# Layer 1's last output share cut at 256 tokens instead of 384

## The chip, the core and the metric

The kernel runs on one core of a Trainium2 chip. The metric is device time in microseconds for one execution. The core has a matrix engine (PE, with its weight loads shown as PEld), a vector engine (DVE), a scalar engine (ACT), GpSimd (POOL), and SyncE (SP), which here issues every DMA. Each engine works through its own instructions in order and waits on semaphores for the others.

## The reference

Two layers act on 512 latent tokens (a grid of 8 rows by 64 columns) and 256 context tokens, of width 1024. A layer normalises and modulates its input, projects it once, and splits the columns among three groups of heads. A is differential attention, B is grouped-query attention, and C is attention to a neighbourhood in the grid plus all context tokens. Each group's result is multiplied by a gate; the results are joined, projected by `w_out`, scaled by `gt` and added to the residual:

```python
yn = neighbourhood_attend(qn, kn, vn.reshape(b, s, C_HEADS, HEAD_DIM), kn_c, vn_c, nat_rpb[l], rows)
yn = yn * jax.nn.silu(gn)
y = jnp.concatenate([ya, yb, yn], axis=-1) @ w_out[l]
...
x = x + gt[:, None] * y
```

After layer 1 only the latent tokens are returned, all of them in float32.

## The kernel before

**Layout.** Activations lie with features on the 128 partitions and tokens along the free axis. Tokens are numbered so that 8 neighbours in a grid column stand together. A float32 product is made of three matmuls: every operand is split into a high and a low part (`yT["h"]`, `yT["l"]` for the joined results, `whi`, `wlo` for the weights), and high x high, high x low and low x high are summed in one PSUM tile. Of the 1024 rows of the joined result, row tiles 0 to 4 belong to groups A and B and tiles 5 to 7 to group C.

**Group C.** `attn(l, "C")` takes the 512 queries in four batches of 128, `j` = 0 to 3, six heads each. To keep a batch's window of keys within 256 tokens, batch `j` < 3 holds tokens 128j + 64 to 128j + 191, and batch 3 holds tokens 448 to 511 and then 0 to 63. This order of queries, 64 to 511 and then 0 to 63, is called the query order here. For each head: scores (L775), bias and maximum on DVE (L824), exponential on ACT (L841), the split into two float16 halves on ACT and POOL (L861, L862), a transpose by DMA from SP into one of four `pt` buffers (L864), and the product with the values on PE (`stage_PV`, L897 and L898, called PV). After three heads DVE divides and joins (L936 to L940), and after six it multiplies by the gate (L942). Then `y_turn` transposes the batch on PE into a PSUM tile `yt` (L618), ACT copies the high part into `yT` (L622) and DVE makes the low part (L623). Batch 3, whose tokens lie at both ends, does this in two pieces of 64 tokens.

**The output of layer 1.** It is made in three steps, all with the residual in `st["part"]`, two tiles (stB, bigC) of four blocks of 128 features. `out_parts` (L1097 to L1099, evacuated at L1127) adds the share of groups A and B for all 512 tokens while group C runs. `out_head` then adds group C's share for tokens 64 to 447, which are the batches 0 to 2: for each of eight feature blocks nine matmuls of 384 tokens into a tile `oh` (`out_n`, L1152 to L1154), an evacuation on DVE (L1163) and a store (L1164). `out_tail` does the same for the first and last 64 tokens after batch 3: four blocks share one PSUM tile `ot`, 36 matmuls of 128 tokens, four evacuations into a tile of their own (L1176), and one store (L1178), twice. `op`, `oh`, `ot` and the projections all draw on one PSUM pool, `psP`, of two buffers; `yt` of group C and the PV tiles draw on another.

**Order.** The Python code issues the program in an order of its own, and a planner then fixes each engine's order: it plays the program through with modelled durations and, whenever an engine is free, takes the instruction that is ready and most urgent. Urgency is the place in the program, less an offset that a few functions are given (stage_S 400). `fill` deals `out_parts` and `out_head` out between the steps of `attn`. By the pace that `both` computes (32 steps of fill, 7 of them kept for the end, over 28 steps of attention), `out_parts` ends with the last but one step, and the first `out_head` is issued in the last one, after the last batch's `y_turn`. So the heads stand behind all of group C in the program, and run earlier only where the planner finds PE free and their inputs there. The order on each engine, SP's included, is then fixed: on the chip an instruction whose input is late holds up what stands behind it.

## Time and profile before

| what | us |
|---|---|
| median of 3 runs | 922.99 (919.12 to 923.62) |
| profiled execution | 921.41 |
| its span, first to last instruction | 919.6 |
| PE busy in the span | 824.1 (90%) |
| DVE busy | 681.9 (74%) |
| ACT busy | 593.1 (64%) |
| POOL busy | 544.1 (59%) |

The profile is of one execution. Times in it count from the start of the span. A line of the timeline gives the start, the duration, the engine and the source line, the operation with output and inputs by the program's names, the shape, how many instructions were merged, and in brackets the idle time of the engine ahead of it with what ended that. "L864" is line 864 of the kernel. A PE row with `128*128 128x384` is a matmul of a full weight tile with 384 tokens. SPq rows are the issue of DMAs by SP.

### The profile page before, as it was taken

The page shows a single profiled execution, that of the slowest core. Times are in us where ns is not written, and L with a number is a line of the kernel's source. Part 1 is how long each engine was busy: PE and PEld are TensorE (multiplying, and loading weights), DVE is VectorE, ACT ScalarE, POOL GpSimd, SP SyncE. Part 2 cuts the span into 40 slices and gives each one's busy share as a digit, 9 for nine tenths or more (in the row PEclk, how much of TensorE's full clock was granted, in tenths as well). Part 3 has the DMA queues.
Part 4 walks back from the last instruction along what each step waited for, and adds up shares of the span by engine and source line. Part 5 has one row for each costly group of instructions (what it writes and reads, how often), then busy time and mean ns, then how long its engine had stood idle before and what let it go on. Part 6 is the DMA issues. An engine that isn't in the chain of part 4 may idle for free. (4 is left out here: it accounts for less than half of the span.)

```text
span 919.6 us, 17947 instructions
## 1 busy us (share of the span) xinstructions
PE 824.1 (90%) x6386; PEld 705.7 (77%) x6386; DVE 681.9 (74%) x1306; ACT 593.1 (64%) x1269; POOL 544.1 (59%) x503
## 2 busy tenths in 40 slices
PE   6898988896998899896999989989959999987988
PEld 3687877795987688784778879978848878875667
DVE  4985787988778866557755798789977976876743
ACT  5334577785887687577663445478758888878630
POOL 1638855899698565434421036939988886654310
PEclk9999998998999999998999989999979999998999
DMA  9924895645879997998798723784547789999642
GB/s 325 320 88 127 202 198 151 139 102 136 190 156 212 223 213 178 223 262 217 145 232 245 246 76 92 173 206 98 123 131 188 133 199 255 205 233 250 129 87 88
DMA packets 307193, 165.46 MB, mean 180 GB/s; under 512 B 256544, under 2 KB 275232, under 8 KB 306976
## 3 DMA queue, kind: packets, MB, share of 16 engines
q1 hardware_dynamic: 307104, 164.33, 74.5%
q8 instruction: 50, 0.82, 0.4%
q14 instruction: 39, 0.32, 0.1%
HBM read 86.55 MB, written 15.47 MB: 111 GB/s over the span
## 5 line engine op out<-in xcount | busy, mean ns | idle before, releaser
L862 POOL TENSOR_TENSOR hl<-p,hl 128x768 f16<-128x768 f32 (+3 forms) x138 | 205.4, 1492 | 170.7 <-ACT hl L861 159.0
L679 PE MATMUL proj<-whi,bigL 128*128 128x384 f32 (+1 forms) x592 | 203.0, 344 | 8.5 <-DVE tb L602 5.1
L680 PE MATMUL proj<-wlo,bigL 128*128 128x384 f32 (+1 forms) x592 | 199.6, 337 | 0.8 <-POOL wlo L92 0.7
L681 PE MATMUL proj<-whi,bigL 128*128 128x384 f32 (+1 forms) x592 | 196.7, 334 | 0.0
L841 ACT ACTIVATE p<-sc,nb,gsc 128x768 f32<-128x768 f32 (+3 forms) x200 | 166.3, 845 | 10.9 <-DVE p L857 4.6
L827 DVE TENSOR_REDUCE mx<-sc 128x1 f32<-128x768 f32 (+2 forms) x128 | 118.6, 931 | 30.3 <-PE sc L775 30.3
L861 ACT CAST hl<-p 128x768 f16<-128x768 f32 (+3 forms) x144 | 104.4, 725 | 46.4 <-DMA pt<-hl 29.9
L679 PEld LDWEIGHTS proj<-whi,bigL 128*128 128x128 f32 x592 | 115.0, 194 | 18.9 <-DVE tb L602 7.2
L680 PEld LDWEIGHTS proj<-wlo,bigL 128*128 128x128 f32 x592 | 115.6, 195 | 3.9 <-POOL wlo L92 1.5
L681 PEld LDWEIGHTS proj<-whi,bigL 128*128 128x128 f32 x592 | 114.5, 194 | 2.7 <-issue 1.6
L92 POOL TENSOR_TENSOR wlo<-raw,whi 128x768 fp32r<-128x768 f32 (+1 forms) x44 | 82.8, 1889 | 31.7 <-ACT whi L89 28.1
L89 ACT CAST whi<-raw 128x768 fp32r<-128x768 f32 (+1 forms) x104 | 80.1, 779 | 25.3 <-DMA raw<-in_w_in_dram 11.1
L897 PEld LDWEIGHTS <-pt 128*128 128x128 f16 x736 | 66.4, 100 | 36.8 <-DMA pt<-hl 23.2
L679 PE MATMUL proj<-whi,bigC 128*128 128x384 f32 (+2 forms) x224 | 75.6, 337 | 1.0 <-ACT xn L462 1.0
L92 DVE TENSOR_TENSOR wlo<-raw,whi 128x768 fp32r<-128x768 f32 (+1 forms) x60 | 61.5, 1028 | 19.4 <-ACT whi L89 18.1
L680 PE MATMUL proj<-wlo,bigC 128*128 128x384 f32 (+2 forms) x224 | 74.3, 332 | 0.0
L163 POOL TENSOR_TENSOR rsqb<-rsqb,half 128x12 f32<-128x12 f32 (+2 forms) x25 | 68.5, 2739 | 9.7 <-DVE rsqb L162 8.8
L681 PE MATMUL proj<-whi,bigC 128*128 128x384 f32 (+2 forms) x224 | 73.6, 331 | 0.0
L898 PEld LDWEIGHTS <-pt 128*128 128x128 f16 x736 | 66.8, 100 | 4.6 <-issue 2.4
L775 PE MATMUL sc<-bigL 128*128 128x512 f16 (+4 forms) x184 | 46.5, 314 | 18.5 <-ACT p L841 18.1
L897 PE MATMUL pv<-vA,pt 128*128 128x128 f16 (+2 forms) x424 | 52.1, 230 | 12.1 <-DMA pt<-hl 12.1
L829 ACT ACTIVATE nb<-mx,lnp,gsc 128x1 f32<-128x1 f32 (+1 forms) x104 | 39.9, 385 | 33.3 <-DVE mx L827 22.5
(327 smaller groups left out, 2038.6 us busy)
## 6 DMA issues: line engine op xcount, KB each, us to landing
raw<-in_w_in_dram SPq DMA_DIRECT2D x64, 384.0 KB, 3.9
adw<-in_w_ada_dram SPq DMA_DIRECT2D x68, 256.0 KB, 3.5
raw<-in_w_out_dram SPq DMA_DIRECT2D x16, 384.0 KB, 4.5
raw<-in_w_in_dram SPq DMA_DIRECT2D x16, 256.0 KB, 3.0
g_d<-tb SPq DMA_DIRECT2D x20, 192.0 KB, 2.8
gt<-g_d SPq DMA_DIRECT2D x18, 192.0 KB, 3.6
hl<-in_w_ada_dram SPq DMA_DIRECT2D x12, 256.0 KB, 4.8
pt<-in_w_ada_dram SPq DMA_DIRECT2D x12, 256.0 KB, 4.9
```

Source lines behind the costliest of these rows:

```text
L89: self.nc.scalar.copy(out=hi, in_=raw2)
L92: self.share("W").tensor_tensor(out=lo, in0=raw2, in1=hi.bitcast(F32), op=ALU.subtract)
L163: G.tensor_tensor(out=y, in0=x, in1=half[:, 0:n], op=ALU.pow)
L679: PE.matmul(ps, lhsT=xh, rhs=hi, start=(kt == 0), stop=False)
L680: PE.matmul(ps, lhsT=xh, rhs=lo, start=False, stop=False)
L681: PE.matmul(ps, lhsT=xl, rhs=hi, start=False, stop=(kt == KT - 1))
L827: V.tensor_reduce(out=mx[:, 0:ns], in_=ps[:, 0:w * ns].rearrange("p (a b) -> p a b", b=w), axis=AX.X, op=ALU.max)
L841: A.activation(out=p[:, w * x:w * x + w], in_=u["ps", i][:, w * x:w * x + w], func=AF.Exp, bias=u["nb", i][:, x:x + 1], scale=lc[l]["sc"][ ...
L861: A.copy(out=hl[:, 0:n], in_=p)
L862: lo_eng.tensor_tensor(out=hl[:, n:2 * n], in0=p, in1=hl[:, 0:n], op=ALU.subtract)
L897: PE.matmul(po[r, :], lhsT=pt[:, b, r], rhs=V_[:, vt, c0:129], start=first, stop=False)
L898: PE.matmul(po[r, 0:65 - c0], lhsT=pt[:, nb + b, r], rhs=V_[:, vt, c0:65], start=False, stop=stop)
```

## The change

In layer 1 group C's result is kept in query order: batch `j` goes to columns 128j of `yT`, batch 3 in one piece. `out_head` takes columns 0 to 255 (batches 0 and 1, tokens 64 to 319) and waits for these two in the program; `out_tail` takes columns 256 to 511 (tokens 320 to 511 and 0 to 63). In the tail two feature blocks share one PSUM tile, each evacuated in two pieces (192 and 64 tokens) into the residual itself, right after its matmuls, and each pair of blocks is stored by two DMAs. The output tensor is in query order, and the host turns it back.

```diff
             if j > 3:
                 spans = [(0, 128, 128 * (j - 4))]
+            elif l + 1 == DEPTH:
+
+                spans = [(0, 128, 128 * j)]
             elif j < 3:
                 spans = [(0, 128, 128 * j + 64)]
...
-                    while any((l, "C", j) not in turned for j in range(3)):
+                    while any((l, "C", j) not in turned for j in range(2)):
...
-        ps = psP.tile([128, 512], F32, tag="p", name="oh")[:, 0:384]
-        out_n(ps, l, db, lambda t: t[:, 64:448], False)
-        dst = st["part", db // 4][:, db % 4, 64:448]
+        ps = psP.tile([128, 512], F32, tag="p", name="oh")[:, 0:256]
+        out_n(ps, l, db, lambda t: t[:, 0:256], False)
+        dst = st["part", db // 4][:, db % 4, 64:320]
         V.scalar_tensor_tensor(out=dst, in0=ps, scalar=mods[l][2][:, db, 0:1], in1=dst, op0=ALU.mult, op1=ALU.add)
-        SP.dma_start(out=out[:, db, 128:512], in_=dst)
+        SP.dma_start(out=out[:, db, 0:256], in_=dst)
...
-        for h in range(2):
+        for h in range(KT // 2):
             ps = psP.tile([128, 512], F32, tag="p", name="ot")
-            p = st["part", h]
-            t = sb([128, 4, 128], F32, "tA", 1)
-            v = [ps[:, 128 * d:128 * d + 128].rearrange("p (a t) -> p a t", a=2) for d in range(4)]
-            for d in range(4):
-                out_n(v[d], l, 4 * h + d, ends, d % 2 == 1)
-            for d in range(4):
-                V.scalar_tensor_tensor(out=t[:, d, :].rearrange("p (a t) -> p a t", a=2), in0=v[d], scalar=mods[l][2][:, 4 * h + d, 0:1],
-                                       in1=ends(p[:, d, :]), op0=ALU.mult, op1=ALU.add)
-            SP.dma_start(out=out[:, 4 * h:4 * h + 4, 0:128], in_=t)
+            for d in range(2):
+                db, v = 2 * h + d, ps[:, 256 * d:256 * d + 256]
+                out_n(v, l, db, lambda t: t[:, 256:512], d == 1)
+                p = st["part", db // 4][:, db % 4, :]
+                for c0, t0, n in ((0, 320, 192), (192, 0, 64)):
+                    V.scalar_tensor_tensor(out=p[:, t0:t0 + n], in0=v[:, c0:c0 + n], scalar=mods[l][2][:, db, 0:1],
+                                           in1=p[:, t0:t0 + n], op0=ALU.mult, op1=ALU.add)
+            p = st["part", h // 2][:, 2 * (h % 2):2 * (h % 2) + 2, :]
+            for c0, t0, n in ((256, 320, 192), (448, 0, 64)):
+                SP.dma_start(out=out[:, 2 * h:2 * h + 2, c0:c0 + n], in_=p[:, :, t0:t0 + n])
```

## The prediction

> **What bounds the kernel now.** I read the busy times by stage first, for the last 40 us, because the diff touches nothing earlier than the fourth batch of group C of layer 1. Columns: stretch; its length; PE, weight load, DVE, ACT and POOL busy; granted clock; DMA share; GB/s.

> ```profile
> core 0: us, PE busy (x) PEld busy (x) DVE busy (x) ACT busy (x) POOL busy (x), PEclk, DMA share, GB/s
> 880.00:887.30 7.30, 7.30 (x51) 5.63 (x49) 2.92 (x7) 2.57 (x6) 2.77 (x3) 1.00 0.45 101
> 887.30:891.00 3.70, 1.91 (x29) 1.45 (x28) 2.13 (x4) 1.03 (x3) 0.91 (x1) 1.00 0.60 135
> 891.00:897.00 6.00, 4.85 (x44) 4.01 (x42) 2.24 (x5) 0.30 (x1) 0.00 (x0) 1.00 0.49 98
> 897.00:907.00 10.00, 10.00 (x61) 9.90 (x60) 5.28 (x11) 0.94 (x3) 0.00 (x0) 1.00 0.27 98
> 907.00:915.00 8.00, 8.00 (x73) 8.00 (x72) 1.75 (x5) 0.00 (x0) 0.00 (x0) 1.00 0.25 84
> 915.00:919.60 4.60, 0.16 (x2) 0.02 (x1) 1.12 (x4) 0.00 (x0) 0.00 (x0) 0.62 0.18 57
> ```

> From 897 to 915 PE is never idle at full clock, while every other engine mostly waits: PE sets the end. Before that it has two holes, 1.8 us in 887.3:891 and 1.15 us in 891:897. The timeline of PE says what they wait for and where the two kinds of closing matmul stand.

> ```profile
> 886.94 0.40 PE L1099 MATMUL op<-bigL,wlo 128*128 128x512 f32 x1
> 889.13 0.52 PE L618 MATMUL yt<-ident,o 128*128 128x128 f32 x3 [1.79 <-DVE o L942]
> 890.95 0.61 PE L1152 MATMUL oh<-bigL,whi 128*128 128x384 f32 x2
> 892.71 0.23 PE L897 MATMUL pv<-vA,pt 128*128 128x129 f16 x1 [1.15 <-DMA pt<-hl]
> 893.20 0.44 PE L1153 MATMUL oh<-bigL,whi 128*128 128x384 f32 x1
> 896.10 0.23 PE L897 MATMUL pv<-vA,pt 128*128 128x129 f16 x1
> 897.36 0.34 PE L1153 MATMUL oh<-bigL,whi 128*128 128x384 f32 x1
> 900.14 0.34 PE L1154 MATMUL oh<-bigL,wlo 128*128 128x384 f32 x1
> 900.32 0.49 PE L618 MATMUL yt<-ident,o 128*128 128x128 f32 x3
> ...
> 907.01 0.22 PE L1152 MATMUL ot<-bigL,whi 128*128 128x128 f32 x1
> ...
> 914.88 0.27 PE L1154 MATMUL ot<-bigL,wlo 128*128 128x128 f32 x1
> ```

> A matmul's own duration (0.34, 0.27) overlaps its neighbours, so cost is read from start to start. From 897.36 to 900.14 lie 16 steps: 0.174 us for a 384-token matmul (later ones 0.176; I take 0.175). From 907.01 to 914.88 lie 71 steps: 0.111 us for a 128-token one. A third of the tokens costs almost two thirds of the time, and weight loads fill that stretch (8.00 of 8.00 us): the short matmul waits for its weights. What a 256-token matmul of this kind costs stands in layer 0's output:

> ```profile
> 447.20 0.28 PE L1097 MATMUL op<-bigC,whi 128*128 128x256 f32 x1
> ...
> 447.55 0.28 PE L1097 MATMUL op<-bigC,whi 128*128 128x256 f32 x1
> ```

> Three steps in 0.35: 0.117 us, the same three operands in the same order.

> **The change, part by part.** Matmul counts stay: heads and tail have 8 blocks x 3 row tiles x 3 = 72 matmuls each.

> 1. Heads, 384 to 256 tokens: 72 x (0.175 - 0.117) = -4.2 us of PE.

> 2. Tail, 128 to 256 tokens: 72 x (0.117 - 0.111) = +0.4 us.

> 3. Heads need the batches 0 and 1 alone. Batch 1's columns are ready when the DVE row below ends, at 880.1; batch 2's at 890.8. The heads stand behind the last batch in the program in both kernels (the loop's new bound changes no place, since all three batches have been issued when the first head is), so they are the work of least urgency, used where the others wait. Up to 887.3 PE is full of L1097 to L1099, so nothing is gained there; but the hole of 1.79 us ahead of batch 2's transpose can now take 15 of them. I take -1.8; bounds: 0 if the planner does not put them there, -2.9 if the second hole goes as well. That one had heads ready already, and stayed, as PV matmuls (L897) were queued in front of the data; I leave it.

> 4. The last batch. Its rows in the timelines of DVE and of ACT, with those of batches 1 and 2 for comparison:

> ```profile
> 879.52 0.55 DVE L623 TENSOR_TENSOR bigL<-yt,bigL 128x384 fp32r<-128x384 f32 x1
> ...
> 890.20 0.56 DVE L623 TENSOR_TENSOR bigL<-yt,bigL 128x384 fp32r<-128x384 f32 x1 [1.21 <-ACT bigL L622]
> ...
> 897.20 0.56 DVE L936 TENSOR_REDUCE o<-pv 128x192 f32<-128x384 f32 x1 [0.28 <-PE pv L898]
> ...
> 898.60 0.56 DVE L942 TENSOR_TENSOR o<-o,gt 128x384 f32<-128x384 f32 x1
> ...
> 901.94 0.36 DVE L623 TENSOR_TENSOR bigL<-yt,bigL 128x192 fp32r<-128x192 f32 x1 [0.39 <-ACT bigL L622]
> ...
> 907.21 0.62 DVE L1163 SCALAR_TENSOR_TENSOR bigC<-oh,mG,bigC 128x384 f32<-128x384 f32 x1 [0.97 <-PE oh L1154]
> 915.20 1.12 DVE L1176 SCALAR_TENSOR_TENSOR tA<-ot,mG,bigC 128x128 f32<-128x128 f32 x4 [2.89 <-PE ot L1154]
> ```
> ```profile
> 889.68 0.48 ACT L622 CAST bigL<-yt 128x384 fp32r<-128x384 f32 x1 [0.91 <-PE yt L618]
> ...
> 900.84 0.32 ACT L622 CAST bigL<-yt 128x192 fp32r<-128x192 f32 x1 [2.67 <-PE yt L618]
> 901.59 0.32 ACT L622 CAST bigL<-yt 128x192 fp32r<-128x192 f32 x1 [0.42 <-DVE bigL L623]
> ```

> Its DVE chain takes 2.1 us, from the last PV's end (897.1) to 899.16. Its y is ready at 902.3 now, 2.0 us after its transpose began at 900.32; heads covered that until 907. With one copy and one subtraction it takes what batch 2 took, 889.13 to 890.76 = 1.6 us. This cover goes. Laying out PE anew: 15 or a few more of the heads' matmuls in the first hole, 3 in the time of the two at 890.95, 25 between 893.2 and 896.1 (2.9 / 0.117), 27 between the last PV and the transpose (3.15 / 0.117): 70 or more of 72. So the heads run out as the transpose starts, near 900.0 to 900.3 (its input is ready at 899.2, so not earlier). The tail's first matmul wants the high part (1.05 us later), the second also the low part: 901.6 to 901.9 for the steady stream, its last start 70 x 0.117 = 8.2 us on, 909.8 to 910.1 against 914.88. Parts 1 to 3 give -5.6; the layout gives -4.8 to -5.1, so what the lost cover costs is +0.5 to +0.8; I take +0.7 (bounds: 0, and the whole 1.6).

> 5. Evacuation. Four 128-token instructions close the program in 1.12 us. After: the last block's two, 192 and 64 tokens. From 342 ns for 128 and 618 for 384 (rows below) 64 more tokens cost 0.07, so 0.41 and 0.27, overlapping by 0.08 as the four do: 0.6 us, -0.5.

> 6. Stores. Tail stores go from two to eight, and two end the program instead of one. The evacuations by line, the stores with size and us to landing, and two loads issued in a row on SP:

> ```profile
> L1163 DVE SCALAR_TENSOR_TENSOR bigC<-oh,mG,bigC x4: 618/618/619, 902.4 to 907.2; 128x384 f32<-128x384 f32 x4
> L1176 DVE SCALAR_TENSOR_TENSOR tA<-ot,mG,bigC x4: 340/340/349, 915.2 to 916.0; 128x128 f32<-128x128 f32 x4
> out_dram<-stB SPq DMA_DIRECT2D x4, 192.0 KB, 1.9
> out_dram<-tA SPq DMA_DIRECT2D x2, 256.0 KB, 2.3
> 872.77 0.47 SPq L965 DMA_DIRECT2D gt<-g_d  x1
> 873.29 0.60 SPq L966 DMA_DIRECT2D gt<-g_d  x1
> ```

> Two issues in a row stand 0.52 us apart on SP; the last store then holds 64 KB instead of 256 KB, and 192 KB land in 1.9 instead of 2.3 us, so 0.4 comes back: +0.1. Bounds: 0, and +0.5 if small ones land no sooner. The six earlier tail stores and the eight of the heads lie under the tail's 8.4 us; without that cover each would cost its 0.5. [...]

> 7. The tail's bank. Each tail tile now holds two blocks of 256 tokens in one PSUM tile, and the first is read before the second's matmuls are issued. If these wait for the reading, each of four tiles stands for the drain (0.16), 0.05, the two reads (0.6) and a signal (0.1, estimated): 0.9 us, 3.6 in all. It is nothing if PE works on the next tile meanwhile, which has a buffer of its own and 9 x 0.117 = 1.05 us of work, just more than 0.9. The planner does take ready work out of order (heads run ahead of the transpose at 900.32, which precedes them in the program), so I take +0.2; bounds 0 and 3.6.

> Sum: -4.2 + 0.4 - 1.8 + 0.7 - 0.5 + 0.1 + 0.2 = -5.1 us. The profiled execution took 921.41 (span 919.6 and 1.8 around it): 916.3. The median of the runs shown is 922.99, from which it would be 917.9; I take the middle, a base of 922.2, and forecast 917.1.

> **Rivals**, on that base.

> Tail in program order: part 7 at its dear end, +3.4 on the sum, 920.5. For it: ACT's second copy at 901.59 waited until DVE had read other columns of the same PSUM tile, so such accesses are put one after the other. Against it: the free second buffer. [...]

> The hole stays: heads are planned after batch 2 as before (the change then does only part of what it says), 1.8 us less, 918.9. For it: the planner's idea of waits differs from the chip's, or there would be no holes.

> Stores ahead of transposes, the slower side. SP works in order, and the last probabilities pass through it:

> ```profile
> 890.12 2.00 SPq L864 DMA_TRANSPOSE pt<-hl  x1
> 892.28 1.21 SPq L864 DMA_TRANSPOSE pt<-hl  x1
> DMA to landing us min/median/max: 2.5/2.6/4.3
> 895.54 5.95 SPq L1164 DMA_DIRECT2D out_dram<-stB  x4
> ```

> Now all head stores stand behind the transpose of 892.28. Earlier heads mean earlier stores; one put ahead of a transpose holds it until that head is done. If both transposes stood behind the last one, heads would run from 893.2 to 899.2, evacuation and issue to 900.2, the second transpose 1.3 later (its own 1.21 and a gap), landing 2.6 after it, PV 0.7 (two took 1.0), the DVE chain 2.1, turn 1.7: the tail would stream from 908.6, 1.6 later than now; with parts 2, 5, 6 and 7 the end moves by +1.8, 924.0. It is slower than before from the point where the last transpose issues after about 899.7. Against it: the planner favours older work, and the transposes are older. A milder form, the last transpose 2 to 3 us late behind one or two stores, costs 1.2 to 2.2 after the 0.8 of slack before 900: 918.3 to 919.3.

> **How the numbers follow.** The forecast 0.56, tail in program order 0.14, the hole stays 0.10, stores ahead 0.07 fully and 0.10 mildly, 0.03 for what I don't see. The forecast's own range is 915.2 (second hole filled too, turn at 899.2) to 919. Runs of one kernel lie 4.5 us apart (919.12 to 923.62), so I say 913.8 to 922.4, which leaves out the full form of stores ahead. A measurement here tells about 0.5%, 4.6 us, from no change; the forecast lies only 0.5 beyond that. Some 0.8 of its share is beyond, and little else: 0.47 faster. Slower by as much needs stores ahead together with the tail in order, or something unseen: 0.08. The rest, 0.45, is within.

> **What would show it.** Head matmuls (oh, 128x256) 0.117 apart, some of them between the last op and batch 2's transpose, that idle time gone; tail matmuls 0.117 apart with no wait for L1176's successors, on two tiles in turn; the tail's first start near 901.5 and its last near 910; a wait of about a microsecond ahead of it on ACT's L622; the last two evacuations in 0.6 us, and 3.3 from their end to the end of the span. Wrong would be: PE waiting on DVE inside the tail, a store between the last transposes of SP, matmuls of 256 tokens at more than 0.125, or a plan that differs before 877.

## The result, and the profile after

The changed kernel takes 915.61 us in the median of 20 runs (912.07 to 921.82), the kernel before 920.84 beside it (917.04 to 923.62). The ratio is 0.9946, with a 95% interval of 0.9931 to 0.9962: 5.0 us less of 921 (3.5 to 6.4). The forecast, 917.1 on a base of 922.2, is a ratio of 0.9945.

The profiled execution of the changed kernel is the slowest of its 20, 921.82 us with a span of 920.0, so its whole span can't be set against the 919.6 of before. Up to the last matmul of `out_parts` (`op`) both kernels issue the same work in the same order, and this matmul starts at 886.94 before and at 891.15 after. All that the change can do lies behind it. The comparison below is therefore the **stretch**, from the start of the last `op` matmul to the end of the span: 919.6 - 886.94 = 32.66 us before, 920.0 - 891.15 = 28.85 us after.

The busy times by stage of the changed kernel, with the columns that the prediction gives for this view:

```profile
core 0: us, PE busy (x) PEld busy (x) DVE busy (x) ACT busy (x) POOL busy (x), PEclk, DMA share, GB/s
891.40:895.00 3.60, 3.60 (x33) 3.58 (x32) 2.63 (x6) 0.65 (x2) 0.19 (x1) 1.00 0.99 101
895.00:901.70 6.70, 6.70 (x76) 5.88 (x74) 3.22 (x8) 0.78 (x2) 0.72 (x1) 1.00 0.65 180
901.70:903.60 1.90, 1.90 (x20) 1.55 (x18) 1.27 (x4) 0.30 (x1) 0.00 (x0) 1.00 0.20 69
903.60:905.80 2.20, 0.53 (x4) 0.31 (x3) 1.00 (x3) 0.48 (x1) 0.00 (x0) 1.00 0.35 119
905.80:908.60 2.80, 2.76 (x12) 2.60 (x13) 0.62 (x2) 0.00 (x0) 0.00 (x0) 0.53 0.02 6
908.60:915.90 7.30, 7.30 (x61) 7.30 (x61) 4.21 (x14) 0.00 (x0) 0.00 (x0) 0.95 0.24 72
915.90:920.00 4.10, 0.29 (x3) 0.08 (x1) 0.61 (x2) 0.00 (x0) 0.00 (x0) 0.95 0.46 128
```

PE has no hole any more from 891.4 to 903.6, where it had two before. In their place stands one stretch, 903.60 to 905.80, in which PE is busy for 0.53 of 2.20 us, and behind it 2.8 us with a granted clock of 0.53. The timeline of PE in the same kernel names both:

```profile
891.15 0.39 PE L1102 MATMUL op<-bigL,wlo 128*128 128x512 f32 x1
891.38 0.28 PE L1155 MATMUL oh<-bigL,whi 128*128 128x256 f32 x1
...
894.49 0.28 PE L1157 MATMUL oh<-bigL,wlo 128*128 128x256 f32 x1
894.62 0.49 PE L618 MATMUL yt<-ident,o 128*128 128x128 f32 x3
...
903.34 0.28 PE L1157 MATMUL oh<-bigL,wlo 128*128 128x256 f32 x1
904.75 0.52 PE L618 MATMUL yt<-ident,o 128*128 128x128 f32 x3 [1.13 <-DVE o L942]
905.84 0.72 PE L1155 MATMUL ot<-bigL,whi 128*128 128x256 f32 x2 [0.57 <-ACT bigL L622]
...
907.02 0.41 PE L1155 MATMUL ot<-bigL,whi 128*128 128x256 f32 x1
907.23 0.41 PE L1156 MATMUL ot<-bigL,whi 128*128 128x256 f32 x1
...
909.37 0.28 PE L1155 MATMUL ot<-bigL,whi 128*128 128x256 f32 x1
...
915.91 0.28 PE L1157 MATMUL ot<-bigL,wlo 128*128 128x256 f32 x1
```

Three readings. Between the last `op` and batch 2's transpose stand 27 head matmuls (three whole heads), and that transpose starts 894.62 - 891.15 = 3.47 us behind the last `op`, where before it was 889.13 - 886.94 = 2.19. The heads run out at 903.6, and PE then waits 1.13 us for DVE's gate of batch 3 and 0.57 us for ACT's copy. And the first 15 steps of the tail take 905.84 to 909.37: 3.53 us, two matmuls of one operand standing 0.21 apart; the last 56 steps, 909.37 to 915.91, take 0.117 each.

SP's timeline of the changed kernel shows what stands between the last transposes:

```profile
893.61 1.21 SPq L864 DMA_TRANSPOSE pt<-hl  x1
894.92 1.52 SPq L1167 DMA_DIRECT2D out_dram<-stB  x3
896.54 2.56 SPq L864 DMA_TRANSPOSE pt<-hl  x2
```

Three head stores go ahead of the last two transposes, the first of which waits from 894.82 to 896.54. DVE's timeline shows a second delay:

```profile
902.89 0.46 DVE L1166 SCALAR_TENSOR_TENSOR bigC<-oh,mG,bigC 128x256 f32<-128x256 f32 x1
...
903.65 0.48 DVE L1166 SCALAR_TENSOR_TENSOR bigC<-oh,mG,bigC 128x256 f32<-128x256 f32 x1
904.05 0.55 DVE L942 TENSOR_TENSOR o<-o,gt 128x384 f32<-128x384 f32 x1
...
905.82 0.56 DVE L623 TENSOR_TENSOR bigL<-yt,bigL 128x384 fp32r<-128x384 f32 x1 [1.21 <-ACT bigL L622]
...
916.23 0.61 DVE L1178 SCALAR_TENSOR_TENSOR bigC<-ot,mG,bigC 128x192 f32<-128x192 f32 x2 [0.45 <-PE ot L1157]
```

Two head evacuations run inside batch 3's chain of divide, join and gate. From the last PV (902.28) to the gate's end (904.60) it takes 2.3 us, 2.1 before.

### The profile page after: what moved, and what is told of

Its sections match the earlier page's. It is cut to its first block, busy times and chain, and to the rows that moved or that the text cites. A ratio compares the mean times of both kernels' runs of the same rounds, so it can differ in the third digit from the quotient of the medians.

```text
span 920.0 us, 17966 instructions
## 1 busy us (share of the span) xinstructions
PE 825.3 (90%) x6386; PEld 707.6 (77%) x6386; DVE 680.6 (74%) x1313; ACT 591.5 (64%) x1268; POOL 542.5 (59%) x503
## 5 line engine op out<-in xcount | busy, mean ns | idle before, releaser
L679 PEld LDWEIGHTS proj<-whi,bigL 128*128 128x128 f32 x592 | 116.7, 197 | 19.0 <-DVE tb L602 6.5
L681 PEld LDWEIGHTS proj<-whi,bigL 128*128 128x128 f32 x592 | 115.9, 196 | 2.7 <-issue 1.6
L897 PEld LDWEIGHTS <-pt 128*128 128x128 f16 x736 | 66.8, 100 | 36.2 <-DMA pt<-hl 22.1
L898 PEld LDWEIGHTS <-pt 128*128 128x128 f16 x736 | 67.0, 101 | 4.7 <-issue 2.2
L897 PE MATMUL pv<-vA,pt 128*128 128x128 f16 (+2 forms) x424 | 52.5, 231 | 10.5 <-DMA pt<-hl 10.3
## 6 DMA issues: line engine op xcount, KB each, us to landing
adw<-in_w_ada_dram SPq DMA_DIRECT2D x68, 256.0 KB, 3.6
raw<-in_w_in_dram SPq DMA_DIRECT2D x16, 256.0 KB, 3.1
g_d<-tb SPq DMA_DIRECT2D x20, 192.0 KB, 2.7
gt<-g_d SPq DMA_DIRECT2D x18, 192.0 KB, 3.4
hl<-in_w_ada_dram SPq DMA_DIRECT2D x12, 256.0 KB, 4.9
pt<-in_w_ada_dram SPq DMA_DIRECT2D x12, 256.0 KB, 5.0
```

Of the source, the lines that this page charges most:

```text
L679: PE.matmul(ps, lhsT=xh, rhs=hi, start=(kt == 0), stop=False)
L681: PE.matmul(ps, lhsT=xl, rhs=hi, start=False, stop=(kt == KT - 1))
L897: PE.matmul(po[r, :], lhsT=pt[:, b, r], rhs=V_[:, vt, c0:129], start=first, stop=False)
L898: PE.matmul(po[r, 0:65 - c0], lhsT=pt[:, nb + b, r], rhs=V_[:, vt, c0:65], start=False, stop=stop)
```

## The experiments

The table holds every kernel that was run. "Timed" is the ratio to runs of the kernel before on the same chip. The other columns come from the profile of one execution each, in us behind the start of its last `op`; "idle" is PE's idle time between the last head and the tail, "slow" the number of the tail's steps, from one matmul's start to the next, of 0.2 us or more. The diffs are against the changed kernel.

| kernel | timed (95%) | stretch | batch 2's turn | last turn | tail, first to last start | idle | slow |
|---|---|---|---|---|---|---|---|
| before | 1 | 32.66 | 2.19 | 13.38 | 20.07 to 27.94 | - | 0 |
| before again | one run | 32.43 | 2.20 | 13.18 | 19.87 to 27.75 | - | 0 |
| after | 0.9946 (0.9931 to 0.9962) | 28.85 | 3.47 | 13.60 | 14.69 to 24.76 | 1.13 + 0.57 | 15 |
| after again | 0.9956 (0.9935 to 0.9978) | 29.17 | 3.42 | 13.61 | 14.70 to 25.06 | 1.13 + 0.57 | 18 |
| after, third | 0.9949 (0.9927 to 0.9971) | 29.15 | 3.41 | 13.54 | 14.63 to 24.98 | 1.13 + 0.57 | 18 |
| cut at 384 | 1.0002 (0.9982 to 1.0022) | 33.91 | 2.19 | 15.50 | 22.19 to 30.06 | - | 0 |
| tail in order | 1.0001 (0.9971 to 1.0031) | 34.08 | 3.42 | 13.56 | 14.64 to 29.93 | 1.14 + 0.57 | 32 |
| heads after turn 2 | 0.9943 (0.9921 to 0.9964) | 27.08 | 2.19 | 12.10 | 14.55 to 22.91 | 0 | 0 |
| stores behind | 0.9928 (0.9908 to 0.9948) | 26.74 | 3.42 | 12.87 | 13.96 to 22.59 | 0.47 + 0.57 | 3 |
| stores behind, again | 0.9941 (0.9916 to 0.9967) | 26.72 | 3.40 | 12.85 | 13.94 to 22.56 | 0.47 + 0.57 | 3 |
| idle time filled | 0.9944 (0.9924 to 0.9963) | 27.63 | 3.42 | 13.60 | 14.69 to 23.53 | 0 | 3 |
| two heads | 0.9939 (0.9910 to 0.9968) | 26.49 | 2.56 | 12.47 | 13.53 to 22.31 | 0.57 | 3 |
| two heads, filled | 0.9927 (0.9898 to 0.9956) | 26.48 | 2.56 | 12.47 | 13.53 to 22.35 | 0 | 3 |

Three slow steps (0.22, 0.37 and 0.22 us) open the tail also in the five profiles that have a granted clock of 1.00 there and no heads left behind the last transpose. The longest of them ends as DVE's low part is there: in the changed kernel that is written by 906.38, and the third matmul starts at 906.43. So three slow steps at the start are not the clock's doing; in the profiles of after, those beyond three are.

**The two kernels again.** Nothing is edited; the question is whether the stretch of one profile is that of the kernel.

> The kernel before as it is, for a second profile. In its first profile the stretch from the start of the last op to the end of the span was 32.66 us, all at full clock. The changed kernel's two profiles have 28.85 and 29.17, which is 3.5 to 3.8 less, while its median gained 4.0 to 5.2. If the first profile is typical, 32.5 to 32.8 again. If PE's idle times of 1.79 and 1.15 us ahead of and behind batch 2's turn can halve its clock as well (the kernel with the cut at 384 showed 0.51 of the clock in the 6 us behind that hole, and a stretch of 33.91), 33.5 to 34.5.

> The changed kernel as it is, for a second profile of it. The prediction's theory (256-token matmuls cost little more than 128-token ones, so 72 of 384 and 72 of 128 become 144 of 256) gives a ratio to before of 0.9946 again, 0.993 to 0.996. In the first profile the first 16 tail matmuls ran 0.213 us apart, the clock at half after PE had been idle 1.13 and 0.57 us; from the start of the last L1102 (op) to the end of the span lay 28.85 us, against 32.66 from the last L1099 before. If the half clock is chance of the phase, it can be absent here, and the same stretch is then about 27.4 us; if it is caused by the idle time each time, the first tail matmuls are slow again and the stretch is 28.5 to 29.

The stretch comes again within 0.3 us: 32.66 and 32.43 before, 28.85 and 29.17 after, each with the same order. The half clock at the tail's start is there again, 18 slow steps in place of 15. Busy times of the second profile of after, for the tail's first 3.67 us and for the stretch at half clock in it:

```profile
core 0: us, PE busy (x) PEld busy (x) DVE busy (x) ACT busy (x) POOL busy (x), PEclk, DMA share, GB/s
903.13:906.80 3.67, 3.58 (x17) 3.38 (x18) 1.15 (x3) 0.00 (x0) 0.00 (x0) 0.60 0.02 4
903.88:907.30 3.42, 3.42 (x17) 3.42 (x18) 0.61 (x2) 0.00 (x0) 0.00 (x0) 0.50 0.02 5
```

17 matmuls take 3.67 us at a mean granted clock of 0.60. The half clock itself lasts 3.42 us and begins 0.75 us behind the tail's start.

**The cut alone.** The query order, the tail's evacuation into the residual, two blocks to a tile and eight stores stay; heads get their 384 tokens and the tail its 128 back.

```diff
-                    while any((l, "C", j) not in turned for j in range(2)):
+                    while any((l, "C", j) not in turned for j in range(3)):
...
-        out_n(ps, l, db, lambda t: t[:, 0:256], False)
+        out_n(ps, l, db, lambda t: t[:, 0:384], False)
...
-                out_n(v, l, db, lambda t: t[:, 256:512], d == 1)
+                out_n(v, l, db, lambda t: t[:, 384:512], d == 1)
...
-                for c0, t0, n in ((0, 320, 192), (192, 0, 64)):
+                for c0, t0, n in ((0, 448, 64), (64, 0, 64)):
```

> Only the cut undone: heads of 384 tokens (batches 0 to 2), tail of 128; query order, batch 3 in one piece, two blocks to a tail tile, eight tail stores all kept. Theory of the prediction: the gain is the cut's, so it goes: 72 x 0.175 + 72 x 0.111 as before, and only about 0.6 us at the last evacuation are kept: ratio 0.999 (0.997 to 1.001), stretch from the last op to the end 31.5 to 32.5 us. Rival, that the other edits (one piece for batch 3, smaller evacuations and stores) bring the gain: ratio 0.994 to 0.996, stretch near 29.

The ratio is 1.0002: without the cut nothing that can be measured is left of the gain. PE's timeline shows the two sizes and the hole as before:

```profile
884.49 0.40 PE L1102 MATMUL op<-bigL,wlo 128*128 128x512 f32 x1
886.68 0.52 PE L618 MATMUL yt<-ident,o 128*128 128x128 f32 x3 [1.79 <-DVE o L942]
...
906.68 0.22 PE L1155 MATMUL ot<-bigL,whi 128*128 128x128 f32 x1
...
914.55 0.28 PE L1157 MATMUL ot<-bigL,wlo 128*128 128x128 f32 x1
```

The tail's 71 steps take 7.87 us, 0.111 each, as before. The stretch of this execution is 1.25 us longer than that of before, and one row of its busy times by stage says why:

```profile
888.50:895.40 6.90, 6.31 (x28) 5.55 (x25) 1.62 (x4) 0.30 (x1) 0.00 (x0) 0.51 0.33 65
```

Behind the hole the clock is granted by half for 6.8 us (888.61 to 895.44), which neither profile of the kernel before shows with the same hole ahead (1.00 in the 10 us from the last `op` on in both). So the same idle time is followed by half clock in one execution and not in another.

**The tail in program order.** Each block's matmuls are put behind those of the block before it, so that PE can't go on with the other tile (`out_n` returns its last matmul for it).

```diff
-                out_n(v, l, db, lambda t: t[:, 256:512], d == 1)
+                if db:
+                    with tc.issue_after(st["tm"].ins):
+                        st["tm"] = out_n(v, l, db, lambda t: t[:, 256:512], d == 1)
+                else:
+                    st["tm"] = out_n(v, l, db, lambda t: t[:, 256:512], d == 1)
```

> The changed kernel, the tail's blocks ordered on PE as the program has them: both blocks of a tile in a row. It prices the rival tail in program order: PE has to wait for DVE's reading of the first block before the second in the same tile, four times 0.8 to 0.9 us, 3.2 to 3.6 in all; time 3.0 to 3.6 above the changed kernel, ratio 0.9985. If matmuls and reading of different columns of a tile could overlap, no wait and the changed kernel's time.

PE's timeline, the four blocks that are second in their tile:

```profile
905.63 0.58 PE L1155 MATMUL ot<-bigL,whi 128*128 128x256 f32 x1 [0.70 <-DVE stB L1183]
...
910.47 0.39 PE L1155 MATMUL ot<-bigL,whi 128*128 128x256 f32 x1 [0.70 <-DVE stB L1183]
...
913.51 0.38 PE L1155 MATMUL ot<-bigL,whi 128*128 128x256 f32 x1 [0.70 <-DVE bigC L1183]
...
916.52 0.39 PE L1155 MATMUL ot<-bigL,whi 128*128 128x256 f32 x1 [0.70 <-DVE bigC L1183]
```

Each sits idle for 0.70 us until DVE has read the other half of its tile. This idle time counts from the modelled end of the matmul before. From start to start the last of these steps, at full clock, takes 0.98 us (915.54 to 916.52) in place of 0.117, so a tile costs 0.86, where the prediction had 0.9, and four cost 3.4. The half clock at the tail's start now lasts 6.8 us (902.73 to 909.55; 0.50 granted in 905.63 to 908.60) in place of 3.4. The stretch is 34.08, 5 us more than after, and the ratio 1.0001: the whole gain of the cut is given back. So part 7's rival was a real mechanism with about the price that the prediction gave it. The edit changes the order alone, so it is the planner's order that spares the changed kernel these waits.

**The hole left empty.** All heads stand behind batch 2's transpose.

```diff
-            PE.transpose(ps[:, 128 * i:128 * i + 128], o[:, 128 * i:128 * i + 128], ident)
+            st["turn", j] = PE.transpose(ps[:, 128 * i:128 * i + 128], o[:, 128 * i:128 * i + 128], ident)
...
-        out_n(ps, l, db, lambda t: t[:, 0:256], False)
+        with tc.issue_after(st["turn", 2].ins):
+            out_n(ps, l, db, lambda t: t[:, 0:256], False)
```

> The changed kernel, head matmuls ordered on PE behind batch 2's turn, as they stood before; the hole ahead of that turn is then empty. The prediction's part 3 (the hole is worth 1.8 us): the turn of batch 3 and the tail come later, ratio 1.8 us above the changed kernel, 0.9965. Rival from the two traces: the 27 head matmuls in the hole held batch 2's turn back by 1.25 us, and with it PV, pt buffers and the last transposes, and they leave PE without work ahead of the tail; without them the heads just reach the last turn, PE waits for nothing there, the tail starts at full clock: stretch from the last op to the end 26.5 to 27.5 us, ratio 0.991 to 0.994, unless the empty hole halves the clock, which gives back up to 1.5.

PE's timeline of this kernel:

```profile
888.02 0.40 PE L1102 MATMUL op<-bigL,wlo 128*128 128x512 f32 x1
890.21 0.52 PE L618 MATMUL yt<-ident,o 128*128 128x128 f32 x3 [1.79 <-DVE o L942]
...
900.12 0.49 PE L618 MATMUL yt<-ident,o 128*128 128x128 f32 x3
...
902.57 0.28 PE L1155 MATMUL ot<-bigL,whi 128*128 128x256 f32 x1
...
910.93 0.28 PE L1157 MATMUL ot<-bigL,wlo 128*128 128x256 f32 x1
```

The hole of 1.79 us is back, and the stretch is still 1.8 to 2.1 us **shorter** than after's: the last transpose comes 1.5 us earlier, heads cover it with no idle time, and the tail runs at full clock (1.00 in 902.57 to 911.00). What the filled hole saves is lost again further on. The timed ratio, 0.9943, can't be told from after's.

**The stores behind the transposes.** Heads stay in the hole; their stores go behind the last transpose on SP.

```diff
-        SP.dma_start_transpose(out=pt[:, 0:n // 64, :], in_=hl[:, 0:2 * n])
+        st["ptT"] = SP.dma_start_transpose(out=pt[:, 0:n // 64, :], in_=hl[:, 0:2 * n])
...
-        SP.dma_start(out=out[:, db, 0:256], in_=dst)
+        with tc.issue_after(st["ptT"].ins):
+            SP.dma_start(out=out[:, db, 0:256], in_=dst)
```

> The changed kernel, the heads' eight stores ordered on SP behind the last transposing DMA (in the first profile three stood ahead of the last two). Theory stores-ahead: the last two transposes issue 1 to 2 us earlier relative to the last op (they were 5.4 and 6.7 us after its start, before the change 3.2 and 5.3), the last turn comes 0.5 to 1.1 us earlier, and the kernel gains that: ratio 0.9935, 0.5 to 1.1 us under the changed kernel. Rival: the transposes were held by their pt buffers, which PV frees late as 27 head matmuls stand ahead of batch 2's turn; then they issue less than 0.5 us earlier and the time is that of the changed kernel within 0.3 us.

> The kernel with the head stores behind the transposes once more, beside the changed kernel on one chip: the first time its stretch was 26.74 us with 3 slow steps. If this was a lucky phase of the clock, idle times of 0.47 and 0.57 us can bring the slow steps back and the stretch is 28; if less idle time keeps the clock, 26.5 to 27.0 again. Ratio to before 0.992 to 0.994, some 2 us under the changed kernel.

SP's and PE's timelines of the first of these two profiles:

```profile
883.52 8.21 SPq L864 DMA_TRANSPOSE pt<-hl  x5
891.78 2.04 SPq L1168 DMA_DIRECT2D out_dram<-stB  x4
```
```profile
884.76 0.40 PE L1102 MATMUL op<-bigL,wlo 128*128 128x512 f32 x1
...
897.63 0.52 PE L618 MATMUL yt<-ident,o 128*128 128x128 f32 x3 [0.47 <-DVE o L942]
...
898.72 0.50 PE L1155 MATMUL ot<-bigL,whi 128*128 128x256 f32 x2 [0.57 <-ACT bigL L622]
...
907.35 0.28 PE L1157 MATMUL ot<-bigL,wlo 128*128 128x256 f32 x1
```

With no store between the transposes the last transpose on PE comes at 12.87 in place of 13.60. This is the price of the three stores: 0.7 us, and PE's wait ahead of that transpose falls with it, from 1.13 to 0.47. The stretch shrinks by more, to 26.74, because with idle times of 0.47 + 0.57 the clock stays whole here (1.00 in 898.71 to 907.36): from the first to the last start of the tail it is 8.63 us (898.72 to 907.35), where after takes 10.07. The second profile agrees in every column.

**The idle time filled.** Nine matmuls ahead of batch 3's transpose and four behind it, into a PSUM tile that nobody reads, keep PE busy where it waits; all else is as in the changed kernel. `st["pvm"]` and `st["turn"]` are the last PV matmul and the last transpose of a batch.

```diff
+            if l + 1 == DEPTH and j == 3:
+                spin(l, 9, st["pvm"])
...
+            if l + 1 == DEPTH and j == 3:
+                spin(l, 4, st["turn"])
...
+    def spin(l, n, after):
+        ps = psS.tile([128, 1024], F32, tag="s", name="wm")
+        with tc.issue_after(after.ins):
+            for i in range(n):
+                PE.matmul(ps[:, 0:256], lhsT=ones.bitcast(F32R), rhs=yT["h"][0][:, 5, 0:256], start=True, stop=True)
```

> The changed kernel with 13 needless matmuls of 256 tokens into a PSUM tile nobody reads: 9 behind the last PV, 4 behind the last turn, so that PE has work in the 1.13 and 0.57 us in which it waited ahead of the tail. Theory clock: the drop to half is caused by that idle time; the tail's steps are then 0.117 us from the first on, and the kernel gains 1.4 us wherever the drop fell: ratio 0.993, up to 1.4 us under the changed kernel. Rival: the drop is chance, or the idle time was too short to matter on average: same time as the changed kernel within 0.3 us, or 0.3 slower by the extra matmuls.

PE's timeline, and the busy times of the tail's first 3.44 us:

```profile
899.57 0.52 PE L618 MATMUL yt<-ident,o 128*128 128x128 f32 x3
899.84 0.70 PE L974 MATMUL wm<-bigL,ones 128*128 128x256 f32 x4
900.66 0.50 PE L1167 MATMUL ot<-bigL,whi 128*128 128x256 f32 x2
...
909.50 0.28 PE L1169 MATMUL ot<-bigL,wlo 128*128 128x256 f32 x1
```
```profile
900.66:904.10 3.44, 3.35 (x26) 3.15 (x27) 1.75 (x5) 0.00 (x0) 0.00 (x0) 1.00 0.14 43
```

The tail starts at the same 14.69 as in after, behind the same transpose at 13.60. But 26 matmuls now fit into 3.44 us, at a granted clock of 1.00, where after needs 3.53 us for 15. The last one starts 1.23 us earlier and the stretch is 1.2 to 1.5 us shorter. So the slow start of the tail, but for its first three steps, is the clock, and in these two kernels the clock goes with the idle time ahead of it. The timed ratio does not show it: 0.9944 beside 0.9956 of the changed kernel on the same chip, with intervals that overlap over most of their width.

**Two heads, and the third profile of after.** Two heads, one fewer than in the changed kernel, are let into the hole, and the stores stand behind the transposes; then the same with four of the idle matmuls. Both diffs are made of the pieces above, with this condition:

```diff
-        out_n(ps, l, db, lambda t: t[:, 0:256], False)
+        with tc.issue_after(st["turn", 2 if db > 1 else 1].ins):
+            out_n(ps, l, db, lambda t: t[:, 0:256], False)
```

> The changed kernel with two heads allowed into the hole (18 matmuls, 2.1 us for a hole of 1.79), the other six behind batch 2's turn, and the head stores on SP behind the last transposing DMA. Theory: batch 2's turn is 0.2 to 0.4 late instead of 1.25, the last turn comes 0.8 to 1.2 us earlier than in the changed kernel, the hole is full and the wait ahead of the tail short, so the clock stays: stretch 25.7 to 26.7 us, ratio 0.991 to 0.992, the best of these. Rival: PE's work sets the start of the tail, not the last turn; then as the kernel with the stores behind, 26.7 and 0.9928.

> The kernel with two heads in the hole and the head stores behind the transposes, and four needless matmuls of 256 tokens behind the last turn, to fill the 0.57 us in which PE waits for ACT there (four slow steps followed it). Theory clock: no slow tail step, 0.3 to 0.4 us under that kernel's stretch of 26.49: 26.0 to 26.3 from the last op to the end; against the changed kernel 2.7 to 3.0 less, ratio to before 0.990 to 0.993. Rival: the four matmuls stand in the way of the tail's start, 0.1 to 0.4 more, 26.6 to 26.9.

> The changed kernel as it is, for a third profile and a ratio beside the two improved ones on one chip. Theory clock: the idle time of 1.13 and 0.57 us ahead of the tail halves the clock every time: 14 to 18 slow steps and a stretch of 28.7 to 29.2. Rival chance: it is absent here, no slow step and about 27.4. Ratio to before 0.994 to 0.997 either way.

The stretch of two heads is 26.49, the shortest with 26.48 of the filled one. Batch 2's transpose is 0.37 late in place of 1.2 to 1.3. Filling the remaining 0.57 us brought nothing of the 0.3 to 0.4 us expected: the clock was whole without it (1.00 in 901.54 to 910.40), and the slow steps that were to go are the first three, which wait for DVE's low part. The third profile of after has the half clock once more. Timed, the best median ratio is 0.9927 (two heads, filled; 0.9898 to 0.9956), and 0.9928 and 0.9941 for stores behind: all of them beat the kernel before, but that they beat the changed kernel, by the 2.1 to 2.7 us of the profiles, lies within the timed intervals and stays unproven.

## Why the prediction was right, and where it failed

The total was right, 0.9945 forecast and 0.9946 measured, but not by the path foretold, and that it fits so closely is in part luck: in the profiled stretch the change brings 3.3 to 3.8 us, not 5.1. Two things happened that the prediction itself named as signs of being wrong, stores between the last transposes of SP and 256-token matmuls at more than 0.125 us. Of the terms:

**Parts 1 and 2 held**, and the cut is what brings the gain. Heads run 0.117 to 0.120 apart (26 steps from 891.38 to 894.49), the tail 0.117 where the clock is whole, 128 tokens 0.111 in the cut at 384. With this cut undone the ratio is 1.0002.

**Part 3 failed as a term, -1.8.** It priced the hole as if the transpose behind it would keep its time. The hole was filled, but with 27 matmuls, 3.2 us of work for 1.79 us of waiting, because the order is fixed by modelled durations; batch 2's transpose and the PV queued behind it came 1.28 us late. And the heads' earlier ends put three stores ahead of the last transposes, which the prediction had only as a rival: its mild form happened, at 0.7 us where 1.2 to 2.2 was forecast. Leaving the hole empty gives no longer stretch (27.08 beside 28.85 to 29.17). With the stores behind the transposes, filling it is worth 0.3 us with three heads (26.74) and 0.6 with two (26.49), by single profiles. The rival "the hole stays" was thus wrong in its sign too: 1.8 us were no loss to it.

**Part 4 held in the tail's start, and failed in the layout ahead of it and in "the steady stream".** The transpose was foretold 13.1 to 13.4 behind the last `op` and came at 13.60; the tail's first start was foretold at 14.7 to 15.0 (901.6 to 901.9 on the clock of before) and came at 14.69. But the heads were to run out as that transpose starts, and they ran out at 903.6, so that PE waited 1.13 us for it: the hole of 1.15 us further up, which the prediction left in place, is gone in the changed kernel, and the three stores held the transpose back (without them the wait is 0.47). From the tail's start on, 0.117 was taken for all steps. PE's idle time ahead of it, 1.13 + 0.57, whose second half the prediction named as the lost cover, was followed by 3.4 us at half clock (0.50 in 905.95 to 909.36). From the first to the last start the tail takes 10.07 to 10.36 us in the three profiles of after and 8.84 with the idle time filled: 1.2 to 1.5 us that no term held. With it filled the stretch is 27.63, which is 4.8 to 5.0 below that of before and near the forecast sum.

The profile also gives the balance. PE's time for the 144 matmuls falls by 3.8 (parts 1 and 2), half clock gives back 1.2, idle time ahead of the tail falls from 1.79 + 1.15 to 1.13 + 0.57, which is 1.2, and from the last matmul's start to the end it is 4.09 in place of 4.72, 0.6: 4.4 in all against 3.8 measured; the remaining 0.6 lies in the tail's first three steps (0.47 more than three of 0.117) and in the heads' 0.120.

**Part 5 held**: 0.61 us for the last two evacuations (1.12 before).

**Part 6 was on the safe side.** From the end of the last evacuation to the end of the span it is 3.16 us, 3.28 before: -0.1, not +0.1. The stores by size in the changed kernel, with us to landing:

```profile
out_dram<-bigC SPq DMA_DIRECT2D x2, 192.0 KB, 2.0
out_dram<-stB SPq DMA_DIRECT2D x2, 64.0 KB, 1.7
out_dram<-bigC SPq DMA_DIRECT2D x2, 64.0 KB, 1.8
```

64 KB in runs of 256 B land in 1.7 to 1.8 us and 192 KB in runs of 768 B in 2.0: a third of the bytes saves only 0.2 to 0.3 us here.

**Part 7 held at its cheap end.** PE is busy 7.30 of 7.30 us in the tail behind the slow start, with no wait for DVE. The dear end was measured as 0.86 a tile, where 0.9 was forecast. In the kernel with the tail in order PE did wait for DVE's reading of the other half of the same tile, 0.70 us each of four times. The signal in that forecast, 0.1, was the author's estimate; in the profile of before 0.14 us lie between the end of DVE's gate of batch 2 (888.99) and the start of its transpose (889.13). What decided is that the planner goes on with another tile meanwhile, as the prediction expected.

**What stays open.** The timed gain, 5.0 us (3.5 to 6.4), 4.1 and 4.7 in the repeats, is about a microsecond above the 3.3 to 3.8 of the profiled stretches. By the difference of the medians it is 5.2, 3.1 and 3.8, and 3.3 to 3.8 lies inside or at the edge of the intervals, so there may be nothing to explain. The cut at 384 shows that the flow with holes of before can also lose its clock behind a hole, 0.51 granted in 888.50 to 895.40; were that so in some of before's executions, the timed gain would be larger than the profiled one. Neither of the two profiles of before shows it, so this is argued and not shown.

## What to carry to other kernels

Filling a hole on an engine whose order is fixed is worth the hole only if the filling ends when the awaited data arrives: count the instructions put there, see when the work behind the hole now starts, and follow what their results issue on other queues (here three stores ahead of two transposes). A cut pays where a matmul's step hardly grows with its tokens: 128 to 256 tokens cost 0.006 us a matmul here (0.111 to 0.117), while 384 to 256 saves 0.058 (0.175 to 0.117). Look for idle time of PE ahead of a dense run: behind 1.13 + 0.57 us of it the tail of after ran at half clock for 3.4 us in each of three profiles. Price that too, or leave enough independent work there.

## What the runs showed of the hardware that was not expected

Where the half clock begins differs too: it is 14.80, 15.45 and 16.06 us behind the last `op` in the three profiles of after, though the idle time is the same. The hole of 1.79 us was followed by half clock in one execution and not in three others; what decides between them was not shown. Some executions of the changed kernel may then keep their clock, and that would explain why filling the idle time does not show in the timed ratios; no run here shows it.
